# The last pair of experts by rows, its scatter summed in PSUM, and a data-dependent loop moved into its down projection

## The chip, the cores and the metric

The kernel runs on one core of a Trainium2 chip. The metric is the device time of one execution in microseconds; the median of three runs stands for the kernel. A profile is one more execution, taken by the hardware profiler.

## What is computed

One layer of a decoder with 256 tokens of width 1024, in float32: attention and retention, a projection and a LayerNorm, cross-attention and a LayerNorm, then a mixture of 32 experts, of which each token takes 4, and a third LayerNorm (LN3). The change lies in the experts and in LN3:

```python
def step(y, blk):
    e, tok, wt = blk
    xb = xf[tok]
    gate = jnp.minimum(xb @ w_gate[e] + b_gate[e], SWIGLU_LIMIT)
    up = jnp.clip(xb @ w_up[e] + b_up[e], -SWIGLU_LIMIT, SWIGLU_LIMIT)
    hmid = gate * jax.nn.sigmoid(SWIGLU_ALPHA * gate) * (up + 1.0)
    out = hmid @ w_down[e] + b_down[e]
    return y.at[tok].add((out * wt[:, None]).astype(y.dtype)), None
...
x = layer_norm(DEEPNORM_ALPHA * x + f, ln3_g[l], ln3_b[l])
```

Each expert has three matrices of 1024 x 1024, 4 MB each; all 32 experts are loaded, 403 MB in float32.

## The kernel before

The attention part fills the first 260 us or so. Then 16 pairs of experts follow. A pair has up to 64 tokens per expert: the two experts' tokens stand in the two halves of 128 columns, and each matmul (128 rows, 64 columns of tokens, 512 columns of weights) of one expert runs beside the other expert's. A pair is three steps on PE (TensorE): gate, up (both by `ff`) and down, each of 32 matmuls in four groups `kk` over the contraction, and each float32 matmul shows as two records in the trace. Between them DVE (VectorE) and ACT (ScalarE) form gate and up (`gate`, `swiglu`); PE transposes the product in two halves (`h_t`, copied by ACT); ACT scales the result of down by the token's weight (`scaled`). PE then multiplies it with the one-hot matrix `ohT` and DVE adds the product onto `y`, two tiles of 128 tokens x 1024 in SBUF (`scatter`); this happens in the next pair's gate step.

The weights come through one queue, issued by SP (SyncE), into 11 places of 2 MB (`tile8` with `n=2`; one of the places is taken by LN3's gain and bias). A load waits until PE has freed its place, and on one of eight semaphores (DMAHW0 to DMAHW7) that count landed loads, so at most eight loads are out. For the pairs in mid-stream one load is 2 MB, whole rows. For the last pair, up and down come in **columns** (`col_parts`): up in two halves of 512 columns; down in 512, 256 and 256 columns. Each part of up's and down's columns is finished over the whole contraction (`cols_mm`) before the next begins, and each part of down is scaled, scattered and taken into LN3's statistics (`n3.stats`, four bn_stats per token tile) while the next is multiplied.

After that stands `extra()`, a loop (`tc.For_i`) over tokens beyond 64 per expert. Its count `n_extra` is read from data; every engine passes the loop, with waits on all the other engines and on all loads. In the runs here it makes no iteration. Then LN3 (`Norm.finish`): mean and variance, `y` minus mean times gain (`center`), times the inverse deviation plus bias (`scale`), and four stores, from SP and ACT.

The code is written in the order in which each engine is to work (`manual_schedule`); the framework places the instructions on the engines' queues from it. The functions that the change touches:

Of the kernel before, what the change touches and what calls it, by code (L numbers as in the profile page):

```python
# [9 lines left out]
F32 = mybir.dt.float32  # L10
# [9 lines left out]
P = 128  # L20
# [54 lines left out]
def _body(tc, nc, ctx, I, out, dbg):  # L75
# [100 lines left out]
    def fours(w):  # L176

        return w.rearrange("(a p j) d -> p a j d", p=P, j=4)
# [411 lines left out]
    class Norm:  # L590

        def __init__(self, o, g, b, z=None):
            self.o, self.g, self.b, self.z = o, g, b, z
# [19 lines left out]
        def rstd(self, t, n=2):  # L615
            mv = self.mv[:, t, :]
            nc.vector.bn_aggr(out=mv[:, 0:2], in_=self.bs[:, t, 0:n])  # L617
            rsqrt_eps(mv[:, 2:3], mv[:, 1:2], 1)

        def plain(self, t):  # L620
# [7 lines left out]

        def center(self, t):
            for c in range(2):  # L630
                y = self.o[t][:, half[c]]
                nc.vector.scalar_tensor_tensor(out=y, in0=y, scalar=self.mv[:, t, 0:1], in1=self.g[:, half[c]],  # L632
                                               op0=ALU.subtract, op1=ALU.mult)

        def scale(self, t, each=None):
            for c in range(2):
# [6 lines left out]
        def finish(self, t, each=None):  # L643
            self.rstd(t, 4)
            self.center(t)
            self.scale(t, each)

    def pair_blocks(a, before_last):

# [306 lines left out]
                                     bias=gb[:, 1, k:k + 1])  # L956
        return xg

    def back(oh, gw):
# [7 lines left out]
        ohT = sm.tile([P, S + 1], F32, name="ohT", tag="ohT", bufs=1)  # L967
# [7 lines left out]

        nc.scalar.activation(out=o, in_=ps, func=AF.Identity, scale=ohT[:, S:S + 1])  # L976

    def pair_mm(ps, lhs, w, kk, c, first, last):

        for k in range(2):  # L980
            for e in range(2):
                r = slice(64 * e, 64 * e + 64)
                nc.tensor.matmul(ps[r, half[c]], lhs[:, 2 * kk + k, r], w(e, k),  # L983
                                 start=(first and k == 0), stop=(last and k == 1))

    def biased(selt, j):
        ps = mm_tile()
        r = slice(64 * j, 64 * j + 64)
        sl = selt[r].rearrange("p e s -> p (e s)")
        for c in range(2):  # L990
            nc.tensor.matmul(ps[:, half[c]], sl, bias[r, half[c]], start=True, stop=False)
        return ps

    def ff(xg, selt, j, get, mid=None):
        ps = biased(selt, j)
        for kk in range(4):
            w = get()
            for c in range(2):
                pair_mm(ps, xg, lambda e, k: w[e][:, k, half[c]], kk, c, False, kk == 3)
            done()  # L1000
            if kk == 0 and mid:
                mid()
        return ps

    def gate(ps, g=None):
# [5 lines left out]

    def swiglu(ps, g, cs=(0, 1)):
        for c in cs:
            p = ps[:, half[c]]
# [24 lines left out]
        scaled(o, ps, ohT)  # L1039
        return o  # L1040

    def scatter(o, ohT, cs=half, after=None):
        for c in cs:
            for t in range(2):
                py = tr_tile()[:, 0:c.stop - c.start]
                nc.tensor.matmul(py, ohT[:, tok[t]], o[:, c], start=True, stop=True)  # L1046
                nc.vector.tensor_tensor(out=y[t][:, c], in0=y[t][:, c], in1=py, op=ALU.add)  # L1047
                if after:
                    after(t, c)


    wpos = [NPRE]
# [1 line left out]
    loads = []  # L1054
    got = []

    for pr in range(1, NPAIR):
# [5 lines left out]
    def col_parts(n, c0, cn, k0, *ks):  # L1063

        for a, b in zip(ks, ks[1:]):
            for e in range(2):
                yield e, lambda t, a=a, b=b: t[:, k0 + a:k0 + b, :], \
                    fours(I[n][0, NE - 2 + e])[:, a // 4, a % 4:a % 4 + b - a, c0:c0 + cn]


    for c in range(2):
        loads.append(([KC, 512], [*col_parts("w_up", 512 * c, 512, 0, 0, 4, 8)]))
    loads.append(([KC, 512], [*col_parts("w_down", 0, 512, 0, 0, 4, 6, 8)]))
    loads.append(([2 * KC, 256], [*col_parts("w_down", 512, 256, 0, 0, 4, 8),
                                  *col_parts("w_down", 768, 256, KC, 0, 4, 6, 8)]))

    def load_double():

        shape, parts = loads.pop(0)
        ts = [tile8(shape, weight=True, n=2) for _ in range(1 + max(e for e, _, _ in parts))]  # L1080
        got.extend(ts)
        for e, dst, src in parts:
            nc.sync.dma_start(out=dst(ts[e]), in_=src)

    def pump_doubles():
        while loads and doubles() >= 1 + max(e for e, _, _ in loads[0][1]):
            load_double()

    def next_double():
# [32 lines left out]
    def static_back(oh, pr):  # L1122
        return back(oh, G[:, :, 2 * pr:2 * pr + 2])

    y = []

    def init_y():

# [46 lines left out]
    def extra():  # L1175

        with tc.For_i(0, n_extra, 1) as i:  # L1177
# [14 lines left out]
            oh = masks(pst)  # L1192
            selt = pick(sst)
            xg = gather(oh, as_t(ta))
            ohT = back(oh, gst)
            count = [0]

            def getter(n):
# [6 lines left out]
                    return ws[j:j + 2]  # L1205
                return get

            g = gate(ff(xg, selt, 0, getter("w_gate")), tb)
            u = swiglu(ff(xg, selt, 1, getter("w_up")), g)
            scatter(down(h_t(u, as_t(ta)), getter("w_down"), ohT, tb), ohT, after=n3.stats)  # L1210

    LN3 = {}

# [38 lines left out]
    def cols_mm(ps, lhs, w, k0, j0):  # L1252

        for k in range(4):
            for e in range(2):
                r = slice(64 * e, 64 * e + 64)
                nc.tensor.matmul(ps[r, :], lhs[:, k0 + k, r], w[e][:, j0 + k, :],  # L1257
                                 start=(k0 + k == 0 and lhs is not xg), stop=(k0 + k == KC - 1))

    ohT = static_back(oh, NPAIR - 1)  # L1260
    ps = biased(selt, 1)
    hT = tile4([KC, P])
# [10 lines left out]
    n3 = Norm(y, LN3["gb"][:, 0, :], LN3["gb"][:, 1, :])  # L1273
    o = tile4([D])
    o_v = out.rearrange("(t p) d -> p t d", p=P)
    for c0, n in ((0, 512), (512, 256), (768, 256)):
        cs = slice(c0, c0 + n)
        ps = mm_tile()[:, 0:n]
        if c0 < 768:
            w = next_double()  # L1280
        for k0 in range(0, KC, 4):
            cols_mm(ps, hT, w, k0, k0 + (KC if c0 == 768 else 0))
        if c0 != 512:
            free8(*w)
# [43 lines left out]
```

## Time and profile before

| | us |
|---|---|
| median of three runs | 1183.12 (1183.11 to 1184.32) |
| the profiled execution | 1185.23 |
| its span, first to last instruction | 1183.3 |
| PE busy / DVE busy / ACT busy | 1124.9 / 323.8 / 233.9 |

Busy times are shares of the span; the profiled execution is 1.9 us longer than its span, and 2.1 us longer than the median of the runs. The chain that ended last covers only the last 10 us of the profile, DVE's, so the stretch before it has to be read from the timeline.

### The profile page before, as it was taken

How to read it: one execution, taken by the hardware profiler on the slowest of the kernel's cores; microseconds unless marked ns; L12 is line 12 of the kernel's file. 1: busy time of each engine (PE TensorE's matmuls, PEld its weight loads, DVE VectorE, ACT ScalarE, POOL GpSimd, SP SyncE). 2: the span in 40 equal slices, each digit the busy share in tenths (PEclk: the TensorE clock that was granted, in tenths of full speed). 3: DMA queues.
4: the chain of work that ended last, by engine and by line, in shares of the span. 5: the costliest groups of instructions: out<-in, count | busy, mean ns of one | idle time of the engine just before them, and what ended most of it. 6: DMA issues, size and time to landing. Idle time of an engine off the chain costs nothing. (4 is left out here: it accounts for less than half of the span.)

```text
span 1183.3 us, 12818 instructions
## 1 busy us (share of the span) xinstructions
PE 1124.9 (95%) x5473; PEld 558.4 (47%) x5473; DVE 323.8 (27%) x461; ACT 233.9 (20%) x433; POOL 28.5 (2%) x37
## 2 busy tenths in 40 slices
PE   8999999999999999999999998989899989999985
PEld 6788899864333434343343434343334343433332
DVE  5666866662121110112110101010101010102114
ACT  5543455431010101010111011010011010120100
POOL 0102300100000000000000000000000000000000
PEclk9999999999989999999999999999999999989998
DMA  9937538589999999999999999999999999999994
GB/s 333 388 125 280 183 133 320 185 349 415 417 397 417 431 425 429 427 428 428 428 428 427 429 426 428 428 427 430 425 429 427 426 430 425 430 427 428 414 372 141
DMA packets 60928, 447.66 MB, mean 378 GB/s; under 512 B 5186, under 2 KB 10050, under 8 KB 35524
## 3 DMA queue, kind: packets, MB, share of 16 engines
q1 hardware_dynamic: 60484, 446.15, 91.7%
q8 instruction: 45, 0.74, 0.3%
q10 hardware_dynamic: 384, 0.66, 0.2%
q14 instruction: 15, 0.12, 0.0%
HBM read 445.73 MB, written 1.05 MB: 378 GB/s over the span
## 5 line engine op out<-in xcount | busy, mean ns | idle before, releaser
L983 PE MATMUL mm<-t,t 128*64 128x512 f32 x2944 | 670.0, 602 | 21.6 <-DMA t<-in_w_up_dram 18.3
L983 PEld LDWEIGHTS mm<-t,t 128*64 128x64 f32 x2944 | 217.6, 138 | 445.9 <-issue 406.7
L1047 DVE TENSOR_TENSOR t<-t,tr 128x512 f32<-128x512 f32 (+1 forms) x66 | 44.2, 670 | 376.0 <-PE tr L1046 376.0
L256 PE MATMUL mm<-t,t 128*128 128x512 f32 (+1 forms) x368 | 129.4, 352 | 1.1 <-ACT t L142 1.1
L257 PE MATMUL mm<-t,t 128*128 128x512 f32 (+1 forms) x368 | 127.0, 345 | 1.0 <-DVE t L143 1.0
L258 PE MATMUL mm<-t,t 128*128 128x512 f32 (+1 forms) x368 | 126.7, 344 | 0.0
L955 ACT ACTIVATE t<-tr,gb 128x128 f32<-128x128 f32 x128 | 48.2, 456 | 259.4 <-PE tr L951 240.4
L143 DVE TENSOR_TENSOR t<-t,t 128x1024 fp32r<-128x1024 f32 (+2 forms) x74 | 86.3, 1181 | 31.2 <-ACT t L142 30.7
L1015 DVE TENSOR_SCALAR mm<-mm 128x512 f32<-128x512 f32 x32 | 22.4, 699 | 216.0 <-PE mm L983 202.7
L142 ACT CAST t<-t 128x1024 fp32r<-128x1024 f32 (+1 forms) x76 | 73.8, 999 | 37.7 <-DVE t L143 15.0
L1008 ACT ACTIVATE t<-mm 128x1024 f32<-128x1024 f32 x16 | 16.4, 1024 | 301.7 <-DVE mm L1007 301.7
L256 PEld LDWEIGHTS mm<-t,t 128*128 128x128 f32 x368 | 69.8, 190 | 12.1 <-ACT t L142 2.7
L257 PEld LDWEIGHTS mm<-t,t 128*128 128x128 f32 x368 | 69.8, 190 | 9.5 <-DVE t L143 2.1
L258 PEld LDWEIGHTS mm<-t,t 128*128 128x128 f32 x368 | 69.8, 190 | 8.3
L1046 PE MATMUL tr<-t,ohT 128*128 128x512 f32 (+1 forms) x132 | 62.6, 605 | 2.0 <-ACT t L976 1.4
L951 PEld LDWEIGHTS tr<-oh,t 128*128 128x128 f32 x512 | 58.4, 192 | 12.6 <-issue 12.2
L951 PE MATMUL tr<-oh,t 128*128 128x128 f32 x512 | 61.4, 278 | 0.0
L1007 DVE TENSOR_SCALAR mm<-mm 128x1024 f32<-128x1024 f32 x16 | 19.7, 1233 | 152.1 <-PE mm L983 152.1
L976 ACT ACTIVATE t<-mm,ohT 128x1024 f32<-128x1024 f32 (+2 forms) x18 | 18.3, 1019 | 213.6 <-PE mm L983 196.5
L1046 PEld LDWEIGHTS tr<-t,ohT 128*128 128x128 f32 x132 | 21.1, 188 | 43.4 <-issue 19.8
L1025 PE MATMUL tr<-ident,t 128*128 128x128 f32 x128 | 23.6, 307 | 17.1 <-ACT t L955 15.5
L1257 PE MATMUL mm<-t,t 128*64 128x512 f32 (+1 forms) x160 | 28.8, 511 | 1.6 <-DVE t L1016 1.6
(166 smaller groups left out, 471.8 us busy)
## 6 DMA issues: line engine op xcount, KB each, us to landing
t<-in_w_gate_dram SPq DMA_DIRECT2D x60, 2048.0 KB, 35.0
t<-in_w_up_dram SPq DMA_DIRECT2D x56, 2048.0 KB, 34.0
t<-in_w_down_dram SPq DMA_DIRECT2D x56, 2048.0 KB, 31.7
t<-in_w_up_dram SPq DMA_DIRECT2D x16, 1024.0 KB, 10.5
t<-in_w_in_dram SPq DMA_DIRECT2D x12, 1024.0 KB, 14.2
t<-in_w_down_dram SPq DMA_DIRECT2D x10, 1024.0 KB, 11.4
t<-in_w_gate_dram SPq DMA_DIRECT2D x8, 1024.0 KB, 7.0
t<-in_w_down_dram SPq DMA_DIRECT2D x10, 512.0 KB, 10.9
```

The source lines that it names most:

```text
L142: h(out=hi, in_=src)
L143: l(out=lo, in0=src, in1=hi.bitcast(F32))
L256: nc.tensor.matmul(ps, lh, rh, start=start, stop=False)
L257: nc.tensor.matmul(ps, lh, rl, start=False, stop=False)
L258: nc.tensor.matmul(ps, ll, rh, start=False, stop=stop)
L951: nc.tensor.matmul(px[:, c, :], zn[t][:, chunk(4 * j + c)], oh[:, t, :], start=(c == 0 and t == 0), stop=(c == 3 and t == 1))
L955: nc.scalar.activation(out=xg[:, k, :], in_=px[:, c, :], func=AF.Identity, scale=gb[:, 0, k:k + 1], bias=gb[:, 1, k:k + 1])
L983: nc.tensor.matmul(ps[r, half[c]], lhs[:, 2 * kk + k, r], w(e, k), start=(first and k == 0), stop=(last and k == 1))
L1025: nc.tensor.transpose(ph[:, c, :], u[:, cols(4 * j + c)], ident)
L1046: nc.tensor.matmul(py, ohT[:, tok[t]], o[:, c], start=True, stop=True)
L1047: nc.vector.tensor_tensor(out=y[t][:, c], in0=y[t][:, c], in1=py, op=ALU.add)
L1257: nc.tensor.matmul(ps[r, :], lhs[:, k0 + k, r], w[e][:, j0 + k, :], start=(k0 + k == 0 and lhs is not xg), stop=(k0 + k == KC - 1))
```

## The change

- The last pair's up and down are loaded and multiplied by rows as in the other pairs. Up's second half and down's first come as four loads of 1 MB each, down's second half as two of 1 MB, two of 0.5 MB and four of 0.25 MB.
- In the middle of up (`kk == 1`), PE copies `y` into two PSUM tiles `ys` by a matmul with the identity (`y_sums`). After down, ACT scales the first half of the result and DVE the second; PE adds the four scatter products onto `ys`. The four DVE adds onto `y` in SBUF go.
- `extra()` stands in the code after the second group of the last pair's down projection, and its body adds onto `ys` too.
- LN3 reads `ys`: the first token tile's statistics by two bn_stats of 512 on DVE; the second's by two passes on ACT with sums (`Norm.sums`, `rstd_of`).

```diff
-        def stats(self, t, cs):
-            for q in range(cs.start // 256, cs.stop // 256):
-                nc.vector.bn_stats(out=self.bs[:, t, q, :], in_=self.o[t][:, 256 * q:256 * q + 256])
+        def stats(self, t, c):
+            nc.vector.bn_stats(out=self.bs[:, t, c, :], in_=self.src[t][:, half[c]])
...
+        def sums(self, t, s):
+            mv = self.mv[:, t, :]
+            nc.scalar.activation(out=self.o[t], in_=self.src[t], func=AF.Identity, accum_out=s[:, 0:1])
+            nc.vector.tensor_scalar_mul(out=mv[:, 0:1], in0=s[:, 0:1], scalar1=1.0 / D)
+            nc.vector.tensor_scalar_mul(out=mv[:, 3:4], in0=s[:, 0:1], scalar1=-1.0 / D)
+            nc.scalar.activation(out=self.o[t], in_=self.src[t], func=AF.Square, bias=mv[:, 3:4],
+                                 accum_out=s[:, 1:2])
+
+        def rstd_of(self, t, s):
+            mv = self.mv[:, t, :]
+            nc.vector.tensor_scalar_mul(out=mv[:, 1:2], in0=s[:, 1:2], scalar1=1.0 / D)
+            rsqrt_eps(mv[:, 2:3], mv[:, 1:2], 1)
...
+    kks = (0, 2, 0, D), (2, 4, 0, D)
     for pr in range(1, NPAIR):
-        for n in ("w_gate", "w_up", "w_down")[:3 if pr < NPAIR - 1 else 1]:
+        for n in ("w_gate", "w_up", "w_down"):
             for a in range(2):
-                for e in range(2):
-                    loads.append(([4, D], [(0, lambda t: t, fours(I[n][0, 2 * pr + e])[:, a])]))
+                if pr == NPAIR - 1 and (n, a) in (("w_up", 1), ("w_down", 0)):
+                    loads.append([*parts(n, pr, a, *kks)])
+                elif pr == NPAIR - 1 and n == "w_down":
+                    loads.append([*parts(n, pr, a, kks[0], (2, 3, 0, D), (3, 4, 0, 512), (3, 4, 512, D))])
+                else:
+                    for e in range(2):
+                        loads.append([(0, lambda t: t, fours(I[n][0, 2 * pr + e])[:, a])])
...
-    for c in range(2):
-        loads.append(([KC, 512], [*col_parts("w_up", 512 * c, 512, 0, 0, 4, 8)]))
-    loads.append(([KC, 512], [*col_parts("w_down", 0, 512, 0, 0, 4, 6, 8)]))
-    loads.append(([2 * KC, 256], [*col_parts("w_down", 512, 256, 0, 0, 4, 8),
-                                  *col_parts("w_down", 768, 256, KC, 0, 4, 6, 8)]))
...
+    def y_sums():
+        ys.extend(mm_tile() for _ in range(2))
+        for t in range(2):
+            for c in half:
+                nc.tensor.matmul(ys[t][:, c], ident, y[t][:, c], start=True, stop=False)
+
+    u = swiglu(ff(xg, selt, 1, stream_get, {1: y_sums}), g)
+    hT = h_t(u, cs=(0,))
+    ps = mm_tile()
+    for kk in range(4):
+        w = stream_get()
+        for c in range(2):
+            pair_mm(ps, hT, lambda e, k: w[e][:, k, half[c]], kk, c, kk == 0, kk == 3, ks=(0,))
+        for c in range(2):
+            pair_mm(ps, hT, lambda e, k: w[e][:, k, half[c]], kk, c, kk == 0, kk == 3, ks=(1,))
+        done()
+        if kk == 0:
+            h_t(u, hT, (1,))
+        if kk == 1:
+            manual.close()
+            extra()
+            manual.enter_context(tc.manual_schedule())
+    o = tile4([D])
+    scaled(o[:, half[0]], ps[:, half[0]], ohT)
+    nc.vector.tensor_scalar_mul(out=o[:, half[1]], in0=ps[:, half[1]], scalar1=ohT[:, S:S + 1])
+    n3 = Norm(y, LN3["gb"][:, 0, :], LN3["gb"][:, 1, :], src=ys)
+    for t in range(2):
+        for c in half:
+            nc.tensor.matmul(ys[t][:, c], ohT[:, tok[t]], o[:, c], start=False, stop=True)
     for c in range(2):
-        for i in range(2):
-            if i == 0:
-                w = next_double()
-            cols_mm(ps[:, half[c]], xg, w, 4 * i, 4 * i)
-            if (c, i) == (1, 0):
-                h_t(g, hT, (0,))
-        free8(*w)
-        swiglu(ps, g, (c,))
-    h_t(g, hT, (1,))
...
-    for c0, n in ((0, 512), (512, 256), (768, 256)):
...
-        scaled(o[:, cs], ps, ohT)
-        scatter(o, ohT, (cs,), n3.stats)
-    manual.close()
-    extra()
-    for t in range(2):
-        n3.finish(t, each=lambda t, c: (nc.sync, nc.scalar)[c].dma_start(out=o_v[:, t, half[c]],
-                                                                         in_=y[t][:, half[c]]))
+        n3.stats(0, c)
+    n3.rstd(0)
+    n3.center(0)
+    n3.sums(1, s3)
+    n3.scale(0, store)
+    n3.rstd_of(1, s3)
+    n3.center(1)
+    n3.scale(1, store)
+    manual.close()
```

The order of instructions on PE at the end of the kernel before (`t_657_5362` and `t_658_5363` are the weights of down's second half, L1046 is the scatter, L1177 the loop; behind the branches stands the loop's body):

```order
L1257 MATMUL mm<-t_657_5362,t_5407 64x256
L1257 MATMUL mm<-t_658_5363,t_5407 64x256
L1046 MATMUL tr<-t_5458,ohT 128x256 x2
L1177 COMPARE_AND_BRANCH
L1177 UNCONDITIONAL_BRANCH x2
```

PE's work was all ahead of the loop. In the changed kernel the loop (L1183) stands on PE behind the first matmul of down's second group (`t_653_5324` is a weight tile of down's first half, L1033 the second transposes):

```order
L990 MATMUL mm<-t_653_5324,t_5443 64x512
L990 MATMUL mm<-t_654_5325,t_5443 64x512
L1033 MATMUL tr<-ident,t_5384 128x128 x4
L990 MATMUL mm<-t_653_5324,t_5443 64x512
L1183 COMPARE_AND_BRANCH
L1183 UNCONDITIONAL_BRANCH x2
L1353 BRANCH_PREFETCH_HINT
```

Of down's 32 matmuls, 9 stand ahead of the loop and 23 behind it. On SP, with the semaphores that each instruction waits for, the kernel before has all loads ahead of the loop:

```order
L1083 DMA t_658_5363<-in_w_down_dram 128x2x256 [waits DMAHW7_49]
L1083 DMA t_657_5362<-in_w_down_dram 128x2x256 [waits DMAHW0_49]
L1083 DMA t_658_5363<-in_w_down_dram 128x2x256 [waits DMAHW1_49]
L1177 COMPARE_AND_BRANCH
L1177 UNCONDITIONAL_BRANCH [waits DMAHW0_49,DMAHW1_49,DMAHW2_49,DMAHW3_49,DMAHW4_49,DMAHW5_49,DMAHW6_49,DMAHW7_49]
```

Where the loop ends on SP in the changed kernel, seven loads follow, of down's second half (3 of its 4 MB; the first 1 MB stands ahead of the loop):

```order
L1183 UNCONDITIONAL_BRANCH [waits DMAHW1_49,DMAHW0_49,DMAHW2_49,SP_sequencer_49,DMAHW3_49,DVE_sequencer_49,DMAHW4_49,PE_sequencer_49,DMAHW5_49,Activation_sequencer_49,DMAHW6_49,Pool_sequencer_49,DMAHW7_49,DVE_49,Pool_49,PE_49,Activation
L1089 DMA t_658_5359<-in_w_down_dram 128x2048
L1089 DMA t_657_5358<-in_w_down_dram 128x1024
L1089 DMA t_658_5359<-in_w_down_dram 128x1024
L1089 DMA t_657_5358<-in_w_down_dram 128x512
L1089 DMA t_658_5359<-in_w_down_dram 128x512
L1089 DMA t_657_5358<-in_w_down_dram 128x512
L1089 DMA t_658_5359<-in_w_down_dram 128x512
L1315 DMA out_dram<-t_2263 128x512 [waits DVE_49]
```

The branch at the loop's end waits for every engine and for all loads issued before. The copies of `y` stand on PE between up's second and third group:

```order
L990 MATMUL mm<-t_645_5263,t_5220 64x512
L990 MATMUL mm<-t_646_5265,t_5220 64x512
L1283 MATMUL mm<-t_2263,ident 128x512 x2
L1283 MATMUL mm<-t_1620,ident 128x512 x2
L990 MATMUL mm<-t_649_5283,t_5220 64x512
L990 MATMUL mm<-t_650_5284,t_5220 64x512
```

Nothing stood between these groups before; up had its columns there.

## Rows read from the trace of the kernel before

**Rows 1.** Busy time by stretch, with the PE clock granted, DMA share, GB/s.

```profile
1066.70:1120.47 53.77, 52.73 (x251) 20.75 (x250) 8.45 (x12) 6.67 (x15) 0.00 (x0) 1.00 1.00 423
...
1131.00:1151.10 20.10, 16.93 (x80) 6.36 (x80) 5.24 (x6) 2.07 (x5) 0.00 (x0) 1.00 1.04 380
1151.10:1170.00 18.90, 17.43 (x105) 7.98 (x104) 4.38 (x10) 1.75 (x4) 0.00 (x0) 1.00 0.62 206
```

**Rows 2.** The loop's line: count, ns min/median/max, first and last start.

```profile
L1177 SPq EVENT_SEMAPHORE  x16: 17/22/6363, 1164.6 to 1173.0; - x16
...
L1177 PEldq EVENT_SEMAPHORE  x9: 51/51/51, 1171.7 to 1176.5; - x9
...
L1177 PEldq COMPARE_BRANCH  x1: 3782/3782/3782, 1171.8 to 1171.8; - x1
...
L1177 PEldq COMPARE_BRANCH  x1: 196/196/196, 1176.6 to 1176.6; - x1
...
L1177 DVEq COMPARE_BRANCH  x3: 41/51/61, 1172.6 to 1174.1; - x3
```

**Rows 3.** Timeline (start, us, what, idle before): PE, once SP, once ACT.

```profile
1022.73 8.78 PE L983 MATMUL mm<-t,t 128*64 128x512 f32 x30 [2.56 <-DMA t<-in_w_up_dram]
...
1092.51 7.20 SPq L1083 DMA_DIRECT2D t<-in_w_up_dram  x2
...
1098.53 13.95 PE L983 MATMUL mm<-t,t 128*64 128x512 f32 x64
...
1132.29 7.09 PE L1257 MATMUL mm<-t,t 128*64 128x512 f32 x32
1140.93 3.65 PE L1257 MATMUL mm<-t,t 128*64 128x512 f32 x16 [1.55 <-DVE t L1016]
1144.52 0.75 PE L1025 MATMUL tr<-ident,t 128*128 128x128 f32 x4
1145.20 3.65 PE L1257 MATMUL mm<-t,t 128*64 128x512 f32 x16
1150.47 0.72 PE L1025 MATMUL tr<-ident,t 128*128 128x128 f32 x4 [1.62 <-DVE t L1016]
1151.12 7.09 PE L1257 MATMUL mm<-t,t 128*64 128x512 f32 x32
...
1158.31 0.69 ACT L976 ACTIVATE t<-mm,ohT 128x512 f32<-128x512 f32 x1 [6.50 <-PE mm L1257]
...
1159.05 1.98 PE L1046 MATMUL tr<-t,ohT 128*128 128x512 f32 x4 [0.85 <-ACT t L976]
1160.97 3.67 PE L1257 MATMUL mm<-t,t 128*64 128x256 f32 x32
...
1166.28 3.67 PE L1257 MATMUL mm<-t,t 128*64 128x256 f32 x32
```

**Rows 4.** Timeline of DVE, the last stretch.

```profile
1172.50 0.43 DVE L613 BATCH_NORM_STATS2 bs<-t 128x6 f32<-128x256 f32 x1
1174.23 0.26 DVE L617 BATCH_NORM_AGGREGATE mv<-bs 128x2 f32<-128x24 f32 x1 [1.30 <-issue]
...
1178.88 1.41 DVE L638 SCALAR_TENSOR_TENSOR t<-t,mv,t 128x512 f32<-128x512 f32 x2
```

**Rows 5.** DMA issues at 1092.5 and 1177 us: KB each, us to landing.

```profile
t<-in_w_up_dram SPq DMA_DIRECT2D x1, 1024.0 KB, 32.0
...
out_dram<-t SPq DMA_DIRECT2D x1, 256.0 KB, 2.1
```

**Rows 6.** Lines 608 and 1008: count, ns min/median/max, first and last start.

```profile
L608 DVE BATCH_NORM_STATS2 bs<-t x8: 694/694/695, 132.1 to 243.7; 128x6 f32<-128x512 f32 x8
...
L1008 ACT ACTIVATE t<-mm x16: 1024/1024/1026, 269.9 to 1132.4; 128x1024 f32<-128x1024 f32 x16
```

**Rows 7.** Busy time by stretch, after a wait and around sparse matmuls.

```profile
1022.73:1028.73 6.00, 6.00 (x20) 1.89 (x22) 0.00 (x0) 0.00 (x0) 0.00 (x0) 0.72 1.01 431
1046.50:1055.50 9.00, 9.00 (x23) 2.45 (x24) 0.00 (x0) 1.76 (x3) 0.00 (x0) 0.62 1.00 424
```

More of the change, by code (lines that the diff above doesn't have):

```diff
@@ L957, in gather, with back @@
         return xg
-    def back(oh, gw):
+    def back(oh, gw, ohT=None):
         po = tr_tile()[:, 0:S]
@@ L976, in scaled, with pair_mm, biased @@
         nc.scalar.activation(out=o, in_=ps, func=AF.Identity, scale=ohT[:, S:S + 1])
-    def pair_mm(ps, lhs, w, kk, c, first, last):
-        for k in range(2):
+    def pair_mm(ps, lhs, w, kk, c, first, last, ks=(0, 1)):
+        for k in ks:
             for e in range(2):
                 r = slice(64 * e, 64 * e + 64)
-                nc.tensor.matmul(ps[r, half[c]], lhs[:, 2 * kk + k, r], w(e, k),
+                nc.tensor.matmul(ps[c][r] if isinstance(ps, list) else ps[r, half[c]], lhs[:, 2 * kk + k, r], w(e, k),
                                  start=(first and k == 0), stop=(last and k == 1))
-    def biased(selt, j):
-        ps = mm_tile()
+    def biased(selt, j, ps=None):
+        ps = mm_tile() if ps is None else ps
         r = slice(64 * j, 64 * j + 64)
@@ L990, in biased, with ff @@
         for c in range(2):
-            nc.tensor.matmul(ps[:, half[c]], sl, bias[r, half[c]], start=True, stop=False)
+            nc.tensor.matmul(ps[c] if isinstance(ps, list) else ps[:, half[c]], sl, bias[r, half[c]], start=True, stop=False)
         return ps
-    def ff(xg, selt, j, get, mid=None):
-        ps = biased(selt, j)
+    def ff(xg, selt, j, get, mid=None, ps=None):
+        mids = mid if isinstance(mid, dict) else {0: mid} if mid else {}
+        ps = biased(selt, j, ps)
         for kk in range(4):
@@ L1000, in ff @@
             done()
-            if kk == 0 and mid:
-                mid()
+            if kk in mids:
+                mids[kk]()
         return ps
@@ L1013, in swiglu @@
         for c in cs:
-            p = ps[:, half[c]]
+            p = ps[c] if isinstance(ps, list) else ps[:, half[c]]
             nc.vector.tensor_scalar(out=p, in0=p, scalar1=LIMIT, scalar2=-LIMIT, op0=ALU.min, op1=ALU.max)
@@ L1040, in down, with scatter @@
         return o
-    def scatter(o, ohT, cs=half, after=None):
-        for c in cs:
+    def scatter(o, ohT):
+        for c in half:
             for t in range(2):
-                py = tr_tile()[:, 0:c.stop - c.start]
+                py = tr_tile()
                 nc.tensor.matmul(py, ohT[:, tok[t]], o[:, c], start=True, stop=True)
                 nc.vector.tensor_tensor(out=y[t][:, c], in0=y[t][:, c], in1=py, op=ALU.add)
-                if after:
-                    after(t, c)
     wpos = [NPRE]
@@ L1055, in _body, with parts @@
     got = []
+    def parts(n, pr, a, *pieces):
+        for j0, j1, c0, c1 in pieces:
+            for e in range(2):
+                yield e, lambda t, at=(j0, j1, c0, c1): t[:, at[0]:at[1], at[2]:at[3]], \
+                    fours(I[n][0, 2 * pr + e])[:, a, j0:j1, c0:c1]
+    kks = (0, 2, 0, D), (2, 4, 0, D)
     for pr in range(1, NPAIR):
-        for n in ("w_gate", "w_up", "w_down")[:3 if pr < NPAIR - 1 else 1]:
+        for n in ("w_gate", "w_up", "w_down"):
             for a in range(2):
-                for e in range(2):
-                    loads.append(([4, D], [(0, lambda t: t, fours(I[n][0, 2 * pr + e])[:, a])]))
[L1063 to L1068, printed above, removed]
-    for c in range(2):
-        loads.append(([KC, 512], [*col_parts("w_up", 512 * c, 512, 0, 0, 4, 8)]))
-    loads.append(([KC, 512], [*col_parts("w_down", 0, 512, 0, 0, 4, 6, 8)]))
-    loads.append(([2 * KC, 256], [*col_parts("w_down", 512, 256, 0, 0, 4, 8),
-                                  *col_parts("w_down", 768, 256, KC, 0, 4, 6, 8)]))
+                if pr == NPAIR - 1 and (n, a) in (("w_up", 1), ("w_down", 0)):
[3 more added lines that the diff above has]
+                else:
+                    for e in range(2):
+                        loads.append([(0, lambda t: t, fours(I[n][0, 2 * pr + e])[:, a])])
     def load_double():
-        shape, parts = loads.pop(0)
-        ts = [tile8(shape, weight=True, n=2) for _ in range(1 + max(e for e, _, _ in parts))]
+        pieces = loads.pop(0)
+        ts = [tile8([4, D], weight=True, n=2) for _ in range(1 + max(e for e, _, _ in pieces))]
         got.extend(ts)
-        for e, dst, src in parts:
+        for e, dst, src in pieces:
             nc.sync.dma_start(out=dst(ts[e]), in_=src)
     def pump_doubles():
-        while loads and doubles() >= 1 + max(e for e, _, _ in loads[0][1]):
+        while loads and doubles() >= 1 + max(e for e, _, _ in loads[0]):
             load_double()
@@ L1194, in extra @@
             xg = gather(oh, as_t(ta))
-            ohT = back(oh, gst)
+            ohT = back(oh, gst, tab[:, 2, 0:S + 1])
             count = [0]
@@ L1206, in getter, with halves @@
                 return get
-            g = gate(ff(xg, selt, 0, getter("w_gate")), tb)
-            u = swiglu(ff(xg, selt, 1, getter("w_up")), g)
-            scatter(down(h_t(u, as_t(ta)), getter("w_down"), ohT, tb), ohT, after=n3.stats)
+            def halves():
+                return [tr_tile() for _ in range(2)]
+            ps = ff(xg, selt, 0, getter("w_gate"), ps=halves())
+            for c in range(2):
+                g = tb[:, half[c]]
+                nc.vector.tensor_scalar_min(out=ps[c], in0=ps[c], scalar1=LIMIT)
+                nc.scalar.activation(out=g, in_=ps[c], func=AF.Sigmoid, scale=SWI)
+                nc.vector.tensor_tensor(out=g, in0=ps[c], in1=g, op=ALU.mult)
+            u = swiglu(ff(xg, selt, 1, getter("w_up"), ps=halves()), tb)
+            hT = h_t(u, as_t(ta))
+            ps = halves()
+            get = getter("w_down")
+            for kk in range(4):
+                w = get()
+                for c in range(2):
+                    pair_mm(ps, hT, lambda e, k: w[e][:, k, half[c]], kk, c, kk == 0, kk == 3)
+            for c in range(2):
+                scaled(tb[:, half[c]], ps[c], ohT)
+                for t in range(2):
+                    nc.tensor.matmul(ys[t][:, half[c]], ohT[:, tok[t]], tb[:, half[c]], start=False, stop=False)
+            free8(tab, *ws2)
     LN3 = {}
@@ new lines, in y_sums @@
+    def y_sums():
[6 more added lines that the diff above has]
+    ps = mm_tile()
+    for kk in range(4):
+        w = stream_get()
+        for c in range(2):
+            pair_mm(ps, hT, lambda e, k: w[e][:, k, half[c]], kk, c, kk == 0, kk == 3, ks=(0,))
+        for c in range(2):
+            pair_mm(ps, hT, lambda e, k: w[e][:, k, half[c]], kk, c, kk == 0, kk == 3, ks=(1,))
[6 more added lines that the diff above has]
+            manual.enter_context(tc.manual_schedule())
@@ new lines, in _body @@
+    o = tile4([D])
+    scaled(o[:, half[0]], ps[:, half[0]], ohT)
+    nc.vector.tensor_scalar_mul(out=o[:, half[1]], in0=ps[:, half[1]], scalar1=ohT[:, S:S + 1])
+    n3 = Norm(y, LN3["gb"][:, 0, :], LN3["gb"][:, 1, :], src=ys)
+    o_v = out.rearrange("(t p) d -> p t d", p=P)
+    for t in range(2):
+        for c in half:
+            nc.tensor.matmul(ys[t][:, c], ohT[:, tok[t]], o[:, c], start=False, stop=True)
+    for c in range(2):
+        n3.stats(0, c)
+    n3.rstd(0)
+    n3.center(0)
@@ L1287, in _body @@
+    s3 = sm.tile([P, 2], F32, name="s3", tag="s3", bufs=1)
+    n3.sums(1, s3)
+    store = lambda t, c: (nc.sync, nc.scalar)[c].dma_start(out=o_v[:, t, half[c]], in_=y[t][:, half[c]])
+    n3.scale(0, store)
+    n3.rstd_of(1, s3)
+    n3.center(1)
+    n3.scale(1, store)
     manual.close()
-    extra()
-    for t in range(2):
-        n3.finish(t, each=lambda t, c: (nc.sync, nc.scalar)[c].dma_start(out=o_v[:, t, half[c]],
-                                                                         in_=y[t][:, half[c]]))
```

39 lines of the change are left out of this document (8 added, 31 removed).

## The prediction

> **What bounds the kernel now.** I read three views in this order: the busy time by stretch, the timeline of the last pair, and the instructions of the loop's own line. In a pair in mid-stream [rows 1] the transfers run without a gap (share 1.00, 423 GB/s) and PE is busy for 52.73 of 53.77 us: loads and PE are nearly balanced. In the last pair the column pieces load more slowly, at 380 GB/s, and the question is which of the two ends last. SP's own waits on the loop's line tell it: the first of them, on the landing of the loads, ends at 1164.6 [rows 2], while PE starts its last 32 records at 1166.28 [rows 3]. From 1131 on every wait of PE is put down to DVE or ACT, none to a load [rows 3]. So PE's chain sets the end: up from 1132.29 to 1148.85, down from 1151.12 to 1169.95 [rows 3], then scatter, sum, loop and LN3 on DVE to 1178.88 + 1.41 = 1180.29 [rows 4], and 3.0 us to the span's end at 1183.3 for the last store. The price of the change is read from that chain.
>
> **The change part by part.** I compare the end of the last down matmul, E (1169.95 now), and what follows E.
>
> *Up.* It takes 16.56 us now, with a wait of 1.55 and four transposes that cost 0.68 (1144.52 to 1145.20) inside. Undivided, 64 records take 13.95 [rows 3]. New are four f32 matmuls 128x512 that copy y into PSUM (y_sums). Two such matmuls, four records, keep PE from 1159.05 to 1160.97, 1.92 us [rows 3], so four cost 3.84. Up becomes 17.79, **+1.23**. No work of PE hides them. Their operands are ready: the scatter before is done in the pair's gate step.
>
> *First weights.* The first up step now needs two whole tiles of 2 MB. The first column piece (1 MB) lands now 32.0 us after its issue at 1092.51, at 1124.5 [rows 3, 5]; at 380 GB/s it began at about 1121.7. Two row tiles (4.2 MB) at 423 GB/s end at 1131.6, and PE is there at 1132.29. I cost this at nothing; at 380 GB/s it would be 0.5 us late.
>
> *From up to down.* The gap is 2.27 us now, of which 1.62 is the wait for one half of swiglu [rows 3]; the other half was done earlier. Now both halves stand there, and the down tile takes up's PSUM, so PE waits for both: about 3.1 us, the first transposes within it. **+0.83.**
>
> *Down with the loop inside.* It takes 18.83 now, 4.4 of it for the scatters of the first two parts (1158.21 to 1160.97 and 1164.64 to 1166.28). These go: the new scatter adds onto PSUM after E. In their place: 13.95 for the matmuls, 0.68 for the second transposes, and the loop. No iteration runs (the row of the loop's DVE share before LN3 is a wait of 1.30, [rows 4]), yet each engine passes it. PE's pass can be read whole, because it lies after PE's work now [rows 2]: a first wait at 1171.7, one branch of 3782 ns at 1171.8, the other eight waits up to 1176.5, the last branch of 196 ns at 1176.6. That is 5.1 us, hidden now, since nothing of PE's follows; the same branches cost DVE 41 to 61 ns. In the changed order 23 of the 32 down matmuls stand behind it, so all 5.1 lie on the path. Down becomes 19.73, **+0.90**, and E 1172.9. Its lower bound is DVE's 1.30, its upper one 5.1 plus a slower branch while loads run, which I leave to the range.
> [...]
>
> *SP's queue.* Seven of the sixteen new loads of up's second half and of down, 3.1 MB, stand behind the loop. SP's pass ends when the last engine arrives: now SP waits 6363 ns in one wait, up to 1173.0 [rows 2], which is DVE. In the changed kernel PE and ACT arrive last, at about 1157.8. The transfers, done with the rest by about 1153, stand idle until then. The seven loads begin at 1158.2; a store of 256 KB takes 2.1 us to land [rows 5]; the rest at 380 to 423 GB/s takes 6.8 to 7.6: all are there by 1168. PE needs the last pieces at about 1171, as it is itself held by the branch. Cost nothing, margin 2 to 3 us; without the branch the margin is gone (rival 1).
>
> *The rows themselves.* 16.8 MB at 423 instead of 380 GB/s land 4.5 us earlier. This is worth nothing here, since PE is later than the loads, and the idle stretch at the loop takes it back.
>
> *After E.* Now 10.34 us to the end of DVE, 1.30 of them the loop. New: ACT scales the first half (0.69, [rows 3]), DVE the second beside PE's first matmul; two matmuls 1.92; two bn_stats of 694 ns [rows 6]; about 0.55 for the aggregate, epsilon and the handovers; then four pairs of 1.41 [rows 4] and four tiny DVE operations, 0.15 each, for the second tile's sums. That makes 4.55 + 5.64 + 0.6 = 10.8, **+0.45** (bounds 0 and +1). The DVE adds of y go, the loop's 1.30 goes, and two whole matmuls with their wait come in. ACT's two passes over the second tile, 1.02 each [rows 6], hide beside DVE's first pairs; POOL's power stays beside the subtraction, as now. With ACT later than that, DVE's scale of the second tile would be late next.
>
> *PE's clock.* [...] In 1046.5 to 1055.5, around sparse matmuls, it was 0.62 over 9 us, 3.4 lost [rows 7]. The waits of 1.55 and 1.62 lost nothing: 1.00 all through [rows 1]. PE's new stop of 5.1 us is longer than 2.56, so I take **+1.7**, with 0 (the fall ends within the stop) and 3.4 as ends.
>
> **Sum:** 1.23 + 0.83 + 0.90 + 0.45 + 1.70 = **+5.1 us**. The profiled execution took 1185.23 (span 1183.3); one like it would take 1190.3, span 1188.4. The median of the runs is 1183.12, 2.1 below it, so I forecast **1188.2**. Its own range, with the clock's and the tail's ends: 1186.0 to 1190.5.
>
> **The rivals.**
> 1. *The loop is cheap on PE* (not slower). The branch costs what it costs on DVE, so PE passes in 1.4 us, and no clock is lost. For it: the other engines pass so. Against it: the 3782 ns on PE, over a loop body that has not changed there in kind. PE would resume at about 1159; the first piece behind the loop lands at 1162.2, just when it is needed, the last at 1168, up to 1.2 late. 5.1 - 1.7 - 3.7 = -0.3: **1182.8**, or 1184.0 if the pieces are late. It decides if the branch takes under about 1 us. Chance 0.13.
> 2. *The clock falls twice*, in the gap after up (3.1 us, longer than the 2.56 that did it once) and at the loop. For: that row. Against: four transposes stand within the gap. 1.7 more: **1189.9**. Chance 0.17.
> 3. *The loads behind the loop set the end*: from an empty queue the seven take over 2.4 us longer than I allow, so that even a held PE waits. Each microsecond beyond costs one: about **1189.5**. Nothing in the profile shows such a slow start. Chance 0.06.
> 4. *The loads set the end today*, and the rows give their 4.5 us: **1178.6**. Against: SP's wait ends at 1164.6, before PE's last part starts. Chance 0.04.
> That the change does not do what it says is excluded by the order above: the loop, the copies and the row loads stand where the words put them.
>
> **How the numbers follow.** The forecast gets 0.60. A measurement of this kernel can tell about 0.2%, 2.4 us, from no change: faster is under 1180.8, slower over 1185.5. Faster: rival 4 and a little of rival 1, 0.06. Same: most of rival 1 and the lowest part of the forecast, 0.15. Slower: the rest, 0.79. The range runs from 1183.0, which takes in half of rival 1, to 1190.8, half of rival 2; outside are rival 4, the other halves, about 0.19.
>
> **What would show it.** In the changed profile: PE's long branch on the loop's line, of 3.5 to 4 us, between two down matmuls; a hole in the transfers from about 1153 to 1159; the copies of y, eight records, 3.8 us; a granted clock below 1 right after the loop; E near 1173 to 1175; 10 to 11 us from E to the last DVE operation. I am wrong if the branch is short, if PE waits there for a load, or if the clock stays at 1.00 and E lies at 1170 or before.

## The result and the profile after

The changed kernel takes 1194.18 us (median; four runs, 1192.45 to 1197.46) beside 1183.72 for the kernel before: a ratio of 1.0091, with a 95% interval of 1.0068 to 1.0114. It is slower, as forecast, but by 10.5 us and not by 5.1, above the range. The profiled execution is the slowest of the four, 1197.46 with a span of 1195.7; before it was 1185.23 and 1183.3, so 12.2 us are to be found in the trace.

The timeline of PE in the changed kernel, from the last up step to the last matmul (start, us, what, idle before), stands against [rows 3]:

```profile
1133.22 7.09 PE L990 MATMUL mm<-t,t 128*64 128x512 f32 x32
1140.24 3.70 PE L1283 MATMUL mm<-t,ident 128*128 128x512 f32 x8
1143.87 7.09 PE L990 MATMUL mm<-t,t 128*64 128x512 f32 x32
1152.58 0.72 PE L1033 MATMUL tr<-ident,t 128*128 128x128 f32 x4 [1.62 <-DVE t L1024]
1153.99 5.35 PE L990 MATMUL mm<-t,t 128*64 128x512 f32 x16 [0.70 <-ACT t L1034]
1159.28 0.75 PE L1033 MATMUL tr<-ident,t 128*128 128x128 f32 x4
1159.95 1.07 PE L990 MATMUL mm<-t,t 128*64 128x512 f32 x2
1165.67 1.98 PE L990 MATMUL mm<-t,t 128*64 128x512 f32 x4 [4.65 <-DMA t<-in_w_down_dram]
1170.54 11.81 PE L990 MATMUL mm<-t,t 128*64 128x512 f32 x42 [2.89 <-issue]
1183.13 3.70 PE L1308 MATMUL mm<-t,ohT 128*128 128x512 f32 x8 [0.78 <-ACT t L983]
```

Up is as forecast. Down, from 1153.99 to 1182.35, takes 28.36 us instead of the forecast 19.73. Three things are to be seen in it: two holds, of 4.65 and 2.89 us, and records that are slow. The first 16 take 5.35 us, the last 42 take 11.81.

The first hold is put down to a load by the timeline. The rows of the loop's line (count, ns min/median/max, first and last start) name the branch, as in [rows 2]:

```profile
L1183 SPq EVENT_SEMAPHORE  x16: 17/22/5067, 1145.0 to 1156.1; - x16
L1183 PEldq EVENT_SEMAPHORE  x9: 51/51/51, 1161.1 to 1165.3; - x9
L1183 SPq COMPARE_BRANCH  x3: 38/46/58, 1135.6 to 1161.2; - x3
L1183 DVEq COMPARE_BRANCH  x3: 41/51/61, 1153.3 to 1161.2; - x3
L1183 PEldq COMPARE_BRANCH  x3: 101/192/3301, 1154.2 to 1165.4; - x3
```

PE's branch of 3301 ns, with PE's waits from 1161.1 to 1165.3 around it, fills the hold; the other engines' branches take 38 to 61 ns. The load that the timeline names cannot have held PE: the last load issued ahead of the loop had landed at 1154.9 us, and the first behind it goes out at 1161.4 and takes 5.1 us to land, which is after the hold. The granted clock by stretch (the number ahead of DMA share and GB/s), against [rows 1, 7]:

```profile
1066.70:1120.47 53.77, 52.73 (x252) 20.75 (x252) 8.45 (x12) 6.66 (x15) 0.00 (x0) 1.00 1.01 428
...
1133.22:1150.96 17.74, 17.74 (x73) 5.86 (x72) 1.22 (x1) 1.49 (x4) 0.00 (x0) 1.00 0.91 381
1153.99:1159.30 5.31, 5.31 (x17) 1.70 (x17) 0.00 (x0) 0.00 (x0) 0.00 (x0) 0.68 0.01 3
1165.67:1170.50 4.83, 1.98 (x4) 0.53 (x5) 0.00 (x0) 0.00 (x0) 0.00 (x0) 0.50 1.01 371
1170.54:1182.35 11.81, 11.81 (x42) 4.73 (x41) 0.00 (x0) 0.00 (x0) 0.00 (x0) 0.81 0.06 23
```

The clock falls twice: after the handover from up to down (0.68), and behind the holds, where it is 0.50 and then 0.81 on the mean. The transfers in the same stretch, 40 slices of 0.78 us from 1151, with the queue that brings instructions (q8):

```profile
DMA  4221000000000086999999999710000000000000
GB/s 199 126 105 42 0 0 10 0 0 0 0 0 0 0 157 178 408 429 356 414 414 411 291 298 393 280 52 3 0 0 0 0 0 0 0 0 0 0 0 0
...
q8 instruction: 3, 0.05, 0.6%
```

The transfers pause from about 1154 to 1162, as forecast. Three packets of instructions, 16 KB each, come in down's stretch; the same stretch of the kernel before has one. In the stretch of the long branch (1161.2 to 1164.6), in that of the second hold (1167.6 to 1170.6) and in the rest of down the same view shows one packet each:

```profile
q8 instruction: 1, 0.02, 1.7%
...
q8 instruction: 1, 0.02, 2.0%
...
q8 instruction: 1, 0.02, 0.7%
```

The first runs from 1162.16 to 1163.09, and the branch ends 1.43 us later, at 1164.52. The second runs from 1168.17 to 1169.12, and PE goes on 1.42 us later, at 1170.54. The last stretch on DVE, against [rows 4]:

```profile
1185.15 1.29 DVE L611 BATCH_NORM_STATS2 bs<-mm 128x6 f32<-128x512 f32 x2 [1.29 <-PE mm L1308]
...
1191.22 1.40 DVE L650 SCALAR_TENSOR_TENSOR t<-t,mv,t 128x512 f32<-128x512 f32 x2
```

From the end of the last down matmul, E (1182.35), to DVE's end at 1192.62 it is 10.27 us; forecast 10.8, before 10.34.

### The profile page after: what moved, and what is told of

It is laid out like the page before. It is cut to its first block, busy times and chain, and to the rows that moved or that the text cites. A ratio compares the mean times of both kernels' runs of the same rounds, so it can differ in the third digit from the quotient of the medians.

```text
span 1195.7 us, 12750 instructions
## 1 busy us (share of the span) xinstructions
PE 1136.0 (95%) x5445; PEld 561.9 (47%) x5445; DVE 320.1 (27%) x452; ACT 235.2 (20%) x435; POOL 27.6 (2%) x37
## 5 line engine op out<-in xcount | busy, mean ns | idle before, releaser
L990 PE MATMUL mm<-t,t 128*64 128x512 f32 x3072 | 705.3, 607 | 29.2 <-DMA t<-in_w_up_dram 18.3
L990 PEld LDWEIGHTS mm<-t,t 128*64 128x64 f32 x3072 | 230.0, 139 | 474.1 <-issue 429.8
L1055 DVE TENSOR_TENSOR t<-t,tr 128x512 f32<-128x512 f32 x60 | 41.2, 687 | 358.3 <-PE tr L1054 358.3
L958 PEld LDWEIGHTS tr<-oh,t 128*128 128x128 f32 x512 | 58.4, 192 | 12.5 <-issue 12.2
L983 ACT ACTIVATE t<-mm,ohT 128x1024 f32<-128x1024 f32 (+1 forms) x16 | 17.4, 1086 | 218.5 <-PE mm L990 218.5
L1054 PE MATMUL tr<-t,ohT 128*128 128x512 f32 x120 | 58.4, 618 | 0.0
L1033 PE MATMUL tr<-ident,t 128*128 128x128 f32 x128 | 23.5, 306 | 17.1 <-ACT t L962 15.5
L1033 PEld LDWEIGHTS tr<-ident,t 128*128 128x128 f32 x128 | 17.9, 210 | 21.7 <-ACT t L962 18.4
```

What stands on the lines that cost most here:

```text
L958: nc.tensor.matmul(px[:, c, :], zn[t][:, chunk(4 * j + c)], oh[:, t, :], start=(c == 0 and t == 0), stop=(c == 3 and t == 1))
L990: nc.tensor.matmul(ps[c][r] if isinstance(ps, list) else ps[r, half[c]], lhs[:, 2 * kk + k, r], w(e, k), start=(first and k == 0), stop=(l ...
L1033: nc.tensor.transpose(ph[:, c, :], u[:, cols(4 * j + c)], ident)
```

## The experiments

Theory A: PE's jump past the loop's body must wait until the code there has been fetched. This is the long branch. The second hold is the same thing once more: the code behind the jump runs into a piece that has not been fetched either. The rivals are B, a chance delay of this execution; C, the loop's waits and the loads that start late behind it; and D, that the rest of the change carries half of the loss. Each kernel was timed beside the kernel before on the same chip.

**The changed kernel again** (no edit).

> The changed kernel once more, unedited. Theory A (after the jump past the loop, PE's instructions must be fetched, and the code behind the jump runs into a second piece that is not there either): the same two holds again at the same instructions, a branch of 3.3 to 3.8 us and a stop of about 2.9 us four matmul records later; median 1192 to 1196. Theory B (the second stop is a chance delay of that one execution, such as a late load): the stop is gone or stands elsewhere, and the median is nearer to 1191.

Measured: 1196.64 beside 1184.64 for the kernel before, ratio 1.0101 (1.0081 to 1.0121). The timeline of PE has both holds again, at the same places:

```profile
1151.01 3.65 PE L990 MATMUL mm<-t,t 128*64 128x512 f32 x16 [0.69 <-ACT t L1034]
...
1155.28 1.07 PE L990 MATMUL mm<-t,t 128*64 128x512 f32 x2
1161.29 1.97 PE L990 MATMUL mm<-t,t 128*64 128x512 f32 x4 [4.94 <-DMA t<-in_w_down_dram]
1166.23 11.83 PE L990 MATMUL mm<-t,t 128*64 128x512 f32 x42 [2.97 <-issue]
```

B falls. Here too a packet of instructions lies in each hold: the branch ends 1.42 us after the first packet, the second hold 1.35 us after the second. The clock behind the loop is low again (0.81; 42 records in 11.83), while the 16 records after the handover run at a clock of 1.00 here (3.65): of the two falls, that after the handover does not come every time.

**Padding the body.**

```diff
                     nc.tensor.matmul(ys[t][:, half[c]], ohT[:, tok[t]], tb[:, half[c]], start=False, stop=False)
+            pt = tr_tile()
+            for _ in range(8):
+                nc.tensor.matmul(pt[:, 0:P], ident, ident, start=True, stop=True)
             free8(tab, *ws2)
```

> Eight matmuls more at the end of the loop's body, which is never run here; everything else as in the changed kernel. Only the addresses behind the body move. Theory A: the code behind the jump now lies within one fetched piece, so the stop of 2.9 us four records behind the loop goes, the long branch stays at 3.3 to 3.8; 3 to 4 us faster than the changed kernel, 1190 to 1191.5. Theory B, and theory C (the stop is a wait for the loads behind the loop): no change, 1193 to 1195.

Measured: 1191.74, ratio 1.0051 (1.0033 to 1.0070), 4.9 us below the changed kernel on the same chip. PE's timeline, and the packets of instructions from the start of down to E:

```profile
1158.21 1.07 PE L990 MATMUL mm<-t,t 128*64 128x512 f32 x2
1164.04 13.28 PE L990 MATMUL mm<-t,t 128*64 128x512 f32 x46 [4.76 <-DMA t<-in_w_down_dram]
```

```profile
q8 instruction: 2, 0.03, 0.5%
```

The second hold is gone, though nothing that runs was edited, only the address of what follows. B and C cannot do that. The gain is somewhat over the 3 to 4 us expected. The second packet is still there, from 1166.13 to 1167.09, but PE now runs through it.

**Padding it more** (48 matmuls in place of 8).

> As a_pad, with 48 instead of 8 matmuls more at the end of the loop's body, which is never run here. Theory A1 (a piece that is not there stops PE wherever the code behind the jump runs into it): the end of the fetched piece lies about 40 matmul records behind the loop instead of 4, and the stop of 2.9 us stands there; 1193 to 1196. Theory A2 (the next piece is fetched meanwhile, and only code that reaches its end soon after the jump is stopped): no second stop, as a_pad, about 7 us above the kernel before.

Measured: 1191.55 beside 1184.43, ratio 1.0062 (1.0038 to 1.0087), and no second hold on PE's timeline:

```profile
1163.48 12.86 PE L990 MATMUL mm<-t,t 128*64 128x512 f32 x46 [5.14 <-DMA t<-in_w_down_dram]
```

A1 falls: 46 records run without a stop behind the first hold, although two more packets come in that time (1163.4 to 1176.4 us):

```profile
q8 instruction: 2, 0.03, 0.9%
```

That is what A2 expects: the packets that come while PE has work stop nothing here. Where the end of a piece lies among the 46 records was an estimate made ahead of the run, and no view shows it.

**A small body.** The loop, its place and its waits stay; the loads in the body stand for the three tiles that it still allocates.

```diff
-            xg = gather(oh, as_t(ta))
             ohT = back(oh, gst, tab[:, 2, 0:S + 1])
...
-            ps = ff(xg, selt, 0, getter("w_gate"), ps=halves())
...
-            hT = h_t(u, as_t(ta))
...
+            for w2 in ws2:
+                for e in range(2):
+                    nc.sync.dma_start(out=w2[:, 2 * e:2 * e + 2, :],
+                                      in_=rows(I["w_gate"][0, bass.ds(pr * 2 + e, 1)].rearrange("o k d -> (o k) d"), 0))
```

> The loop's body, which is never run here, is cut from 142 PE instructions of the program to 13; it leaves out the gate, up and down of an overflow expert. The loop, its place, its waits on all engines and loads stay. Theory A: the jump lands in code that PE already has; the branch falls under 0.3 us, the second stop goes too, and some of the clock's loss: 1185 to 1188 (a wait for the loads behind the loop of up to 1.2 us may appear). Theory C (PE is held by the loop's waits and by the loads that start late behind it): 1193 to 1195, as the changed kernel.

Measured: 1186.44, ratio 1.0015 (1.0000 to 1.0031). PE's timeline, its branches on the loop's line, and the clock behind the loop:

```profile
1156.55 1.07 PE L990 MATMUL mm<-t,t 128*64 128x512 f32 x2
1159.34 3.65 PE L990 MATMUL mm<-t,t 128*64 128x512 f32 x16 [1.72 <-issue]
1163.39 7.08 PE L990 MATMUL mm<-t,t 128*64 128x512 f32 x30 [0.40 <-DMA t<-in_w_down_dram]
```

```profile
L1183 PEldq COMPARE_BRANCH  x3: 101/187/310, 1151.0 to 1159.1; - x3
```

```profile
1159.34:1163.39 4.05, 3.65 (x16) 1.05 (x16) 0.00 (x0) 0.00 (x0) 0.00 (x0) 1.00 0.91 357
```

The branch takes 310 ns instead of 3301, the second hold and the clock's fall behind the loop are gone, and a wait of 0.40 us for a load behind the loop appears. PE's nine waits on the loop's line and the late loads are still there (SP has 12 waits on that line in place of 16; the next kernel has all 16), so C falls: ten of the twelve microseconds are in PE's code, and in what holding PE does to its clock.

**A body of middle size** (overflow expert's up and down left out).

```diff
-            u = swiglu(ff(xg, selt, 1, getter("w_up"), ps=halves()), tb)
-            hT = h_t(u, as_t(ta))
-            ps = halves()
...
-                    pair_mm(ps, hT, lambda e, k: w[e][:, k, half[c]], kk, c, kk == 0, kk == 3)
```

> The loop's body, which is never run here, keeps an overflow expert's gather and gate step and leaves out up and down: 64 PE instructions of the program, between the 13 of a_small and the 142 of the changed kernel. If only a near target is at hand, the branch is already long (3.3 to 3.8 us), and a stop can stand anywhere behind it: 6 to 11 us above the kernel before. If the code at hand reaches past 64 instructions, the branch is 0.3 us as in a_small, 1 to 3 us above the kernel before.

Measured: 1187.28 beside 1184.43, ratio 1.0021 (1.0011 to 1.0032). PE's branches on the loop's line:

```profile
L1183 PEldq COMPARE_BRANCH  x3: 101/187/304, 1155.1 to 1163.0; - x3
```

The longest is 304 ns over 64 instructions, where 142 took 3301: by theory A the target is at hand here and not there. In this kernel and the one with the small body the next packet of instructions begins only after the branch has ended; in all eight profiles with a long branch one begins within it, and the branch ends 1.41 to 1.44 us after that packet's end.

**No loop** (the call of `extra()` removed).

> The changed kernel without the loop; the overflow experts' work is left out. Theory A: rows, copies of y, scatter and LN3 together are worth about nothing against the kernel before: up +1.2, start of up +0.9, handover +0.8, clock after the handover +1.7, down without scatters -4.2, tail about 0: 1183.5 to 1185.5, and all the rest of the slowdown is the loop. Theory D (the other parts of the change carry half of the slowdown, by the copies of y and the later start of up): 1188 or more.

Measured: 1183.63, ratio 0.9986 (0.9973 to 0.9999). PE's timeline:

```profile
1154.26 5.35 PE L990 MATMUL mm<-t,t 128*64 128x512 f32 x16 [0.69 <-ACT t L1034]
1159.54 0.75 PE L1033 MATMUL tr<-ident,t 128*128 128x128 f32 x4
1160.21 10.52 PE L990 MATMUL mm<-t,t 128*64 128x512 f32 x48
```

All of the slowdown goes with the loop; D falls. The fall of the clock after the handover (16 records in 5.35) is here too, so the loop is not its cause.

**The kernel before without its loop** (the same call removed there).

> The kernel before without the loop; the overflow experts' work is left out. Theory: only DVE's pass of 1.30 us goes, 1.3 us faster than the kernel before, so that all but the loop of the change costs between 0 and 1 us (a_noloop against this). Rival (the loop's waits on the last loads hold LN3 too): 3 us or more faster.

Measured: 1182.45 beside 1183.87, ratio 0.9984 (0.9973 to 0.9995), 1.4 us, as the theory has it. Beside 0.9986 for the changed kernel without its loop this says that rows, copies, scatter and LN3 together bring nothing that can be measured; the two intervals leave room for about 2 us either way.

**The loop behind the scatter.**

```diff
-        if kk == 1:
-            manual.close()
-            extra()
-            manual.enter_context(tc.manual_schedule())
...
             nc.tensor.matmul(ys[t][:, c], ohT[:, tok[t]], o[:, c], start=False, stop=True)
+    manual.close()
+    extra()
+    manual.enter_context(tc.manual_schedule())
     for c in range(2):
         n3.stats(0, c)
```

> The changed kernel with the loop behind the scatter onto ys, ahead of LN3's statistics, as it stood before (its body still adds onto ys). Theory A: PE's jump and both fetches lie behind PE's work again, so this is the kernel without the loop plus DVE's pass of about 1.3 us: 1184.5 to 1186, within 0.2% of the kernel before. Rival (the loop costs what it costs wherever it stands, through its waits on all engines): 1188 or more.

Measured: 1185.51 beside 1183.87, ratio 1.0007 (0.9998 to 1.0016). PE's branch is as long as ever, and DVE waits for the barrier before its first statistics:

```profile
L1183 PEldq COMPARE_BRANCH  x3: 101/193/3513, 1170.0 to 1177.4; - x3
```

```profile
1173.21 1.29 DVE L611 BATCH_NORM_STATS2 bs<-mm 128x6 f32<-128x512 f32 x2 [3.35 <-PEq L1183]
```

The long branch costs PE nothing there, since nothing of PE's follows. DVE waits 3.35 us, against 1.29 in the changed kernel, so the loop costs about 2.1 us at this place, somewhat more than the 1.3 expected. The same code at another place makes the difference of some 10 us.

**The copies of y in the handover** (on top of the last one).

```diff
-    u = swiglu(ff(xg, selt, 1, stream_get, {1: y_sums}), g)
+    u = swiglu(ff(xg, selt, 1, stream_get, {3: y_sums}), g)
```

> As b_end, and the copies of y into PSUM stand behind up's last group instead of its second. Theory: they fill the 3.0 us in which PE waits for the first half of swiglu and the copy of the transposes, so that 6.66 us of copies and gap become about 5.0, and the clock does not fall after the gap (it cost 1.7 us in three of five profiles): 2 to 3 us below b_end, about 1182.5, and so 0.1 to 0.2% below the kernel before. Rival (up's second half is needed 3.6 us earlier and its loads are not there): PE waits in up, 0 to 1 us below b_end.

Measured: 1183.27, ratio 0.9990 (0.9978 to 1.0002), 2.2 us below the kernel with the loop behind the scatter. PE's timeline:

```profile
1132.35 13.95 PE L990 MATMUL mm<-t,t 128*64 128x512 f32 x64
1146.23 3.70 PE L1283 MATMUL mm<-t,ident 128*128 128x512 f32 x8
1149.77 0.63 PE L1033 MATMUL tr<-ident,t 128*128 128x128 f32 x4
1151.08 3.65 PE L990 MATMUL mm<-t,t 128*64 128x512 f32 x16 [0.68 <-ACT t L1034]
```

```profile
1151.08:1154.73 3.65, 3.65 (x17) 1.13 (x17) 0.00 (x0) 0.00 (x0) 0.00 (x0) 1.00 1.00 400
```

Copies and gap take 4.85 instead of 3.70 and 3.03, and the clock stays up (1.00). This version is 1.1% faster than the changed kernel, and cannot be told from the kernel before.

**LN3's statistics on DVE alone** (on top of the last one).

```diff
-    for c in range(2):
-        n3.stats(0, c)
+    for t in range(2):
+        for c in range(2):
+            n3.stats(t, c)
...
-    n3.sums(1, s3)
...
-    n3.rstd_of(1, s3)
+    n3.rstd(1)
```

> As b_ys3, but the statistics of LN3's second tile by two bn_stats on DVE as well, ACT's two passes and the four tiny DVE operations go. Theory: two bn_stats of 0.65 us more on DVE's chain, about 0.3 us of tiny operations and waits less: 1.0 us slower than b_ys3. Rival (ACT's passes make DVE wait as long as they save): no change or faster.

Measured: 1183.08, ratio 0.9990 (0.9977 to 1.0002): by the runs no difference. In the profiles DVE's last stretch, from its first statistics to its end, is 8.4 us (1171.01 to 1179.39) against 7.5 (1170.82 to 1178.30). That speaks for the expected 1.0, in one execution each; the medians neither show nor exclude it.

The runs that bear on the loop, side by side. The second column is PE's time from the start of the first to the end of the last of the 48 records behind the second transposes, the fourth counts the packets of instructions on q8 from the start of down to E:

| kernel | 48 records, us | longest branch of PE, ns | packets | ratio to before |
|---|---|---|---|---|
| changed | 22.40 | 3301 | 3 | 1.0091 |
| changed, again | 22.78 | 3521 | 3 | 1.0101 |
| body padded, 8 | 19.11 | 3341 | 2 | 1.0051 |
| body padded, 48 | 19.07 | 3721 | 3 | 1.0062 |
| middle body | 13.76 | 304 | 2 | 1.0021 |
| small body | 13.92 | 310 | 1 | 1.0015 |
| no loop | 10.52 | none | 1 | 0.9986 |

In the changed kernel the loop costs PE 11.9 us (22.40 less 10.52): 4.65 for the first hold, 2.89 for the second, and 4.3 for records at a low clock. Padded, it is 8.6; with the small body 3.4.

## Why the prediction was wrong

**What bounds the kernel: right.** PE's chain set the end before, though by less than I read: SP's waits on the landing of the loads run on from 1164.6 to 1165.7, and PE's last part starts at 1166.28. Without the loop both kernels come out alike although the changed one loads by rows, which fits that the faster loads are worth nothing; rows alone were not tried.

**Up, handover, tail: right.** Up was forecast at 17.79 and took 17.74; the handover 3.1 and 3.03; the tail 10.8 and 10.27. Up starts 0.93 us later in this execution than before; over the profiles of the same code its start lies anywhere from 1129.9 to 1134.1, so I put that down to no part of the change. The sum of all parts but the loop is 1.23 + 0.83 + 0.45 and, for down without the loop, 13.95 + 0.68 - 18.83 = -4.20; that makes -1.7 us against the kernel before. The changed kernel without its loop measured a ratio of 0.9986, which is 1.7 us of 1184.64 (interval 0.1 to 3.2). That the two agree to a tenth is luck: the sum leaves out the fall of the clock after the handover, which this run's profile has too and which costs 1.4 to 1.7; with it the sum is about 0, at the edge of the interval.

**"Down with the loop inside": the step that failed.** I read the long branch of [rows 2] rightly and took it over whole: 5.1 us, of which 4.65 came. But I took it as the whole price of the jump. [Rows 2] show a jump after which PE has nothing left to run, so they cannot show what happens to the code behind it. In the changed kernel that code ran for four records and stopped for 2.89 us; I read this as the end of what had been fetched. Two findings speak for this cause: the stop goes when the addresses move (46 records in 13.28 us with the body padded by 8), and while it lasts a packet of instructions comes in (1168.17 to 1169.12). No rival of mine had a second stop.

**"PE's clock": the term that was mis-sized.** I took 1.7 us for one fall, from the one wait of 2.56 us in [rows 3] and the clock of 0.72 over the 6.00 us behind it in [rows 7], which lost 6.00 x 0.28. Behind the holds the 48 records lost 4.3 us. The second fall, after the handover, which I had as rival 2 at 0.17, is the usual case: the 16 records there took 5.05 to 5.35 us in six of the eight profiles with the gap of 3.03 us, 3.65 in two; without the gap, in the two kernels with the copies moved, 3.65 both times. It costs 1.4 to 1.7 us. The holds and the clock together account for the miss: in this execution 1.70 + 4.34 + 4.65 + 2.89 = 13.6, where I had 5.1 + 1.7 = 6.8. In both sums the rest gives 1.7 back: 11.9 beside the 12.2 us between the two profiled executions, and 5.1.

**The branch's cause.** On PE the branch took 3301 to 3721 ns over the long body, in the seven profiles of the changed kernel and its variants that have it, and 304 and 310 ns over the short ones; on DVE the branches of the same line took 41 to 61 ns. A packet of instructions begins within each long branch and ends 1.41 to 1.44 us before the branch does, so I read the branch as a wait for the code at its target. Not every packet goes with a stop: there is none at the packet of 1159.8 us in the straight run of the kernel without the loop, and none in the 46 records of the body padded by 48, while two come. Right behind the jump of the changed kernel there is one, of 2.89 us.

**Rivals 1 and 3.** The cheap branch of rival 1 came about only where the body was cut; then the loads behind the loop were late by 0.31 to 0.40 us, within the 1.2 that I had allowed. In the changed kernel PE never waits for them, so rival 3 falls. The pause of the transfers came as forecast, longer by 2 to 3 us since PE reached the loop later.

What stays open is what makes PE call for the next piece after a jump (in the four profiles with the loop inside down and a long branch, that packet begins 2.1 to 2.6 us after PE's first record behind the loop), and how far the first piece reaches behind the target. Only three positions were tried, of which one was stopped.

## What to carry to other kernels

A loop that never ran still had a price here: on PE the jump past a body of 142 instructions held it for 4.65 us, it stopped again four records later for 2.89 us, and the records behind ran at a low clock, for 4.3 us more. Put such a loop where PE has no work behind it (1.0007 of the time before, in place of 1.0091), or keep its body short (1.0015 with 13 instructions), and don't carry the price of a jump at the end of a program over to a jump in the middle: whatever follows it is part of the price. These stalls on PE were not paid once: look at how long the records behind a stall take.

## What the runs showed of the hardware

- PE's jump past 142 instructions of the program or more took 3.30 to 3.72 us, in seven profiles; past 13 it took 0.310 us and past 64 0.304, in one each. The other engines took 38 to 61 ns over the long body in the changed kernel's profile.
- Eight matmuls that are never run made the kernel faster, by 4.9 us in the medians and 3.3 to 3.7 us in the traces (22.40 and 22.78 less 19.11), by moving the code behind them. With forty-eight the trace shows 19.07.
- A jump of PE that waited went on 1.41 to 1.44 us after the end of a 16 KB packet of instructions, in eight profiles of eight.
- A gap of 3.03 us on PE, with four transposes near its middle, was followed by a granted clock of 0.68 in the changed kernel's profile, and by slow records in six of the eight profiles that have the gap; filled with 3.70 us of copies it left the clock at 1.00. After the 1.72 us hold of the small body the clock stayed at 1.00 too.
